# Gates and branch projections with tokens in the partitions and 512 weight columns a product

## The chip, the cores and the metric

The kernel runs on one core of one Trainium2 chip. The metric is device time of one execution in microseconds (us). The core's engines are TensorE (PE in the profile; PEld is its weight load), VectorE (DVE), ScalarE (ACT), GpSimd (POOL) and SyncE (SP), which here only issues DMAs. Each engine works through its own queue in order; engines wait for one another by semaphores.

## What is computed

One layer of a hybrid backbone over 256 latent tokens (and a prefix of 256 context tokens) with 2048 channels, in fp32. Cut to the part around the change:

```python
D_MODEL, SEQ, D_FF = 2048, 256, 5632          # h_l: 256 x 2048
def merge(h, ya, yb):
    g_a, g_b = jnp.split(jax.nn.sigmoid(h @ w_gate + b_gate), 2, axis=-1)     # w_gate 2048 x 4096
    return (g_a * (ya @ w_proj_gla) + g_b * (yb @ w_proj_diff)) @ w_out       # 1024 x 2048 each; 2048 x 2048
...
mix_l = merge(h_l, gla_out(o_lf + flip(o_lb), gr_l), diff_out(o_diff))
x_new = x + g1 * mix_l
h2_l = modulate(rms_norm(x_new, norm2_w), sh2, sc2)
x_new = x_new + g2 * conv_ffn(h2_l, w_up, conv_w, conv_b, w_down)
```

Ahead of it stand the modulation vectors (`silu(c) @ w_ada`), the input projection, a chunked gated linear attention (its output is `ya`) and a differential attention of eight heads (its output is `yb`).

## The kernel before, in words

**Products.** Every fp32 operand of a large product is split into a rounded high half and the low rest, and a product is made of three: high by high, low by high, high by low. `split` (L207 to L229) does it for a tile of 128x1024 weights: ScalarE copies the high half (L212), VectorE subtracts to get the low half (L219; now and then POOL does). `fetch` (L231) loads the raw tile on SP's queue. There are four raw buffers and three of each half.

**Two forms.** In the column form, `col_tile` (L244 to L278), a 128x128 tile of weights is stationary and the tokens move. The activations lie as [high | low] of 2 x 256 tokens, so the high weights take one product of 512 columns (L270) and the low weights one of 256 (L272). The result has output channels in the partitions, its two 256-column parts still to be added. In the row form, `row_tile` (L284 to L287), 128 tokens are stationary and 512 weight columns move, in three products of 512 columns. The dv part of the input projection (names `dvb`, L285 to L287) and the last product, down (L1386), are in row form; nearly all else is in column form.

**Order.** The kernel is written with a scheduler that simulates the engines and sets the order of each queue; attention has a high priority (L1132, L1136), so its products stand between those of the gates. Where a table or a list forces an order, `after` ties two instructions.

**Gates.** The loop over the eight heads (L1131 to L1151) makes three gate tiles per head in between attention's work, and the rest behind it: 32 tiles, `gate_tile` (L1116 to L1124). Each is one `col_tile` over 16 contraction tiles; ScalarE moves one half of the bank out and adds the gate bias by channel (L1123), VectorE adds the other half (L1124). `GATE_ADA` (L49) says how many modulation steps (`ada_next`, a VectorE dot of 128x1024, L371) go with each.

**Merge.** The projection loop (L1176 to L1193) runs over 16 channel tiles: two column tiles (`pga`, `pgb`), a sigmoid of the two gates (L1181), evacuation (`added`, L281 on ScalarE, L282 on VectorE), multiplication by the gate (L1187, for one branch on VectorE and for the other on POOL), and in `merged` the sum (L1172) and its split (L237, L238) into the places that the output projection reads. The mix loop (L1216 to L1240) is the output projection in column form.

**Places.** `C` are the places of the gates. They are cut from the places of the odd tiles of the high and low activations, which POOL copies away first by a DMA behind each step of the second dv chunk (`X4`, L1045).

Of the kernel before, what the change touches and what calls it, by code (L numbers as in the profile page):

```python
# [18 lines left out]
P = 128  # L19
D = 2048  # L20
# [33 lines left out]
for _n, _w in [("b_ada", 96), ("norm1", 16), ("norm2", 16), ("ba", 8), ("gonorm", 1), ("qnorm", 1),  # L54
               ("knorm", 1), ("donorm", 1), ("b_gate", 32), ("lam", 256), ("conv_w", 3 * 2 * FT),
               ("conv_b", 2 * FT)]:
    _VEC[_n] = (_o, _w)
    _o += _w
# [21 lines left out]
def _lay_out(i):  # L80
# [20 lines left out]
    a["w_in"] = _tiles(w_in, starts)  # L101
    a["w_gate"] = _tiles(np.asarray(i["w_gate"])[0], range(0, 2 * D, P))
    pg, pd = np.asarray(i["w_proj_gla"])[0], np.asarray(i["w_proj_diff"])[0]
    a["w_proj"] = _tiles(np.concatenate([pg, pd], axis=0), range(0, D, P))
    a["w_out"] = _tiles(np.asarray(i["w_out"])[0], range(0, D, P))
# [19 lines left out]
        "donorm": np.asarray(i["diff_onorm_w"])[0][:, None],  # L125
        "b_gate": _vec_tiles(np.asarray(i["b_gate"])[0]),
        "conv_w": np.asarray(i["conv_w"])[0].reshape(3, 2 * FT, P).transpose(2, 0, 1).reshape(P, -1),
# [25 lines left out]
def layer_kernel(tc, I, out):  # L153
# [3 lines left out]
    with es:  # L157
# [853 lines left out]
        with tc.tile_pool(name="diff", bufs=1) as pd:  # L1011
# [11 lines left out]
            def dv_chunk(j):  # L1023
# [7 lines left out]
                for q in turn:  # L1031
# [12 lines left out]
                    if j:  # L1044
                        nc.gpsimd.dma_start(X4[2 * q][:, 2:, :], A[2 * q + 1])  # L1045
                        A[2 * q + 1] = X4[2 * q][:, 2:, :]

            def dq_tile(h):
# [66 lines left out]

            def gate_tile(j):  # L1116
                ada_next(GATE_ADA[len(gates)])
                b = acc_bank("gate")
                col_tile(I["w_gate"][j], A, b)
                if j == len(C):  # L1120
                    C.append(shared(2 * (j // 2) + 1, j % 2, "C").rearrange("p (a t) -> p a t", a=2))
# [8 lines left out]
            dv_chunk(1)  # L1130
            order = [j for k in range(KT) for j in (k, KT + k)]  # L1131
# [18 lines left out]
            while order:  # L1150
                gate_tile(order.pop(0))  # L1151

# [6 lines left out]
        for p in range(NPAIR):  # L1159
# [9 lines left out]
        yap, ybp = [[y[h].rearrange("p (a b) -> p a b", a=2) for h in range(HEADS)] for y in (ya, yb)]  # L1169

        def merged(c, earlier):
            i = V.tensor_tensor(gates[c], gates[c], gates[16 + c], op=ALU.add)  # L1172
            after(i, earlier)
            split_act(A[c][:, 1, :], A[c][:, 0, :], gates[c])

        for c in range(KT):  # L1176
            ba, bb = acc_bank("pga"), acc_bank("pgb")
            col_tile(I["w_proj"][c, :, 0:8, :], yap, ba)
            col_tile(I["w_proj"][c, :, 8:16, :], ybp, bb)
            for j in (c, 16 + c):  # L1180
                sigs.append(S.activation(gates[j], gates[j], AF.Sigmoid))  # L1181
                after(sigs[-1], sigm)
                after(sigs[-1], copied[0])
            for b, j in ((ba, c), (bb, 16 + c)):
                t = p3.tile([P, T], F32, tag="pt", bufs=2, name="pt")
                i = added(t, b)
                (G if j > c else V).tensor_tensor(gates[j], t, gates[j], op=ALU.mult)  # L1187
                if j == c and c:
                    merged(c - 1, i)
            if c < KT - 2:  # L1190
                ada_next(13 / (KT - 2))
        merged(KT - 1, i)
        ada_done(0)  # L1193

# [7 lines left out]
        def unnormed(k, product, summed):  # L1202
# [10 lines left out]
            after(i, product)  # L1213

        half = KT // 2
        for c in range(KT):  # L1216
            b = acc_bank("mix")
            if 0 < c < half:
                ada_next(1)
            col_tile(I["w_out"][c], A, b)  # L1220
            if c == half:
# [213 lines left out]
```

## Time and profile before

| | us |
|---|---|
| median of 3 runs (lowest 1675.17, highest 1676.67) | 1675.4 |
| the profiled execution | 1675.7 |
| its span, first to last instruction | 1673.9 |
| TensorE busy | 1657.2 |
| VectorE busy | 1279.7 |
| ScalarE busy | 898.4 |
| POOL busy | 338.7 |

The chain of work that ended last is 90% TensorE's. By the first and last start of their products, the gates lie at 527.6 to 758.1 us, up to 694 us between attention's products, the branch projections at 758.3 to 847.9, the output projection (mix) at 848.2 to 937.8, up at 973.6 to 1429.5 and down at 1429.6 to 1668.8.

How to read it: the profile records one execution. A duration on PE is from the issue of a product to a modelled end, so that those of successive products overlap; what a stream of products takes is seen in their starts. "Idle before" names the instruction whose end released the engine. Durations of one instruction are in ns, times in us.

### The profile page before, as it was taken

Reading aid. Unit: us, or ns where it says so; the run is one execution under the profiler, and the core shown is the slowest. Engines: PE = TensorE matmul, PEld = TensorE weight load, DVE = VectorE, ACT = ScalarE, POOL = GpSimd, SP = SyncE. Lnnn points to the kernel's source line nnn. Section 1 sums busy time; section 2 is a strip of 40 time slices with the busy share of each in tenths; the row PEclk is TensorE's granted clock in tenths of the full one; section 3 lists DMA queues with packets and bytes.
Section 4 is the critical chain, followed back from the end, with each engine's and each line's share of the span. In section 5 each row is a group of like instructions: output and inputs, shape, how many; then the busy total and the mean of one; then the engine's idle time right before and its main releaser. Section 6 shows DMA issues by size and latency. Waiting matters only on the chain.

```text
span 1673.9 us, 25645 instructions
## 1 busy us (share of the span) xinstructions
PE 1657.2 (99%) x9476; PEld 1409.6 (84%) x9476; DVE 1279.7 (76%) x2013; ACT 898.4 (54%) x1475; POOL 338.7 (20%) x412
## 2 busy tenths in 40 slices
PE   9999999999999999999999999999999999999998
PEld 6679888788878888888888998888888888888887
DVE  5887877768678888788888797888888888744544
ACT  5235355654456776556655575555555555433332
POOL 0011332415011000002214101221222122684000
PEclk9999999999999999999999999999999999999999
DMA  9996735336665556687877666777777676777764
GB/s 384 408 363 218 228 129 172 113 120 199 200 218 179 187 192 195 226 289 259 270 270 232 178 202 208 238 229 232 237 240 240 220 236 214 209 220 207 219 192 136
DMA packets 111965, 372.74 MB, mean 223 GB/s; under 512 B 14560, under 2 KB 19680, under 8 KB 111840
## 3 DMA queue, kind: packets, MB, share of 16 engines
q1 hardware_dynamic: 102112, 362.51, 66.3%
q0 software_dynamic: 5696, 4.24, 1.0%
q10 hardware_dynamic: 4032, 4.37, 0.8%
q8 instruction: 74, 1.21, 0.3%
q14 instruction: 51, 0.42, 0.1%
HBM read 364.73 MB, written 2.10 MB: 219 GB/s over the span
## 4 chain that ended last, share of the span: by engine, by line
PE 90%; DVE 4%; DMA 3%; ACT 1%; POOL 1%; issue 1%; DVEq 0%; SPq 0%; ACTq 0%
PE down L1386 14%; PE upg L270 9%; PE upv L270 9%; PE gate L270 7%; PE upv L272 5%; PE upg L272 5%; PE sweep L383 4%; PE gate L272 4%; PE mix L270 4%; PE mix L272 2%; PE pga L270 2%; PE pgb L270 2%; PE dvb L285 1%; PE dvb L287 1%; PE dvb L286 1%; PE dq L270 1%
## 5 line engine op out<-in xcount | busy, mean ns | idle before, releaser
L212 ACT CAST whi<-wraw 128x1024 fp32r<-128x1024 f32 (+3 forms) x502 | 514.5, 1028 | 420.6 <-PE down L1386 138.9
L219 DVE TENSOR_TENSOR wlo<-wraw,whi 128x1024 fp32r<-128x1024 f32 (+3 forms) x466 | 562.9, 1209 | 205.7 <-ACT whi L212 200.5
L270 PE MATMUL upg<-x,whi 128*128 128x512 f32 x656 | 229.4, 392 | 0.0
L270 PE MATMUL upv<-x,whi 128*128 128x512 f32 x656 | 229.4, 392 | 0.0
L1386 PE MATMUL down<-whi,g 128*128 128x512 f32 x704 | 216.8, 389 | 0.0
L272 PE MATMUL upv<-x,wlo 128*128 128x256 f32 x656 | 183.0, 280 | 0.0
L272 PE MATMUL upg<-x,wlo 128*128 128x256 f32 x656 | 182.8, 280 | 0.0
L270 PE MATMUL gate<-x,whi 128*128 128x512 f32 x512 | 179.8, 398 | 0.0
L371 DVE CUSTOM_DVE_ANT_0 araw<-araw,cb 128x1024 f32<-128x1024 f32 x128 | 161.2, 1263 | 14.2 <-DMA araw<-in_w_ada 14.0
L219 POOL TENSOR_TENSOR wlo<-wraw,whi 128x1024 fp32r<-128x1024 f32 x36 | 86.8, 2411 | 396.3 <-ACT whi L212 396.3
L1386 PEld LDWEIGHTS down<-whi,g 128*128 128x128 f32 x704 | 132.1, 188 | 27.3
L270 PEld LDWEIGHTS upv<-x,whi 128*128 128x128 f32 x656 | 122.4, 187 | 26.8
L270 PEld LDWEIGHTS upg<-x,whi 128*128 128x128 f32 x656 | 122.4, 187 | 26.8
L272 PE MATMUL gate<-x,wlo 128*128 128x256 f32 x512 | 140.7, 285 | 0.2 <-DVE wlo L219 0.2
L1386 PE MATMUL down<-wlo,g 128*128 128x512 f32 x352 | 137.0, 389 | 0.0
L1297 DVE SCALAR_TENSOR_TENSOR C<-C,vec 128x255 f32<-128x255 f32 x88 | 105.5, 1201 | 36.8 <-ACT C L1296 36.8
L272 PEld LDWEIGHTS upv<-x,wlo 128*128 128x128 f32 x656 | 124.0, 189 | 0.5
L272 PEld LDWEIGHTS upg<-x,wlo 128*128 128x128 f32 x656 | 124.0, 189 | 0.5
L270 PEld LDWEIGHTS gate<-x,whi 128*128 128x128 f32 x512 | 94.3, 188 | 19.9 <-issue 0.7
L272 PEld LDWEIGHTS gate<-x,wlo 128*128 128x128 f32 x512 | 96.4, 189 | 5.6 <-issue 2.6
L270 PE MATMUL mix<-x,whi 128*128 128x512 f32 x256 | 88.8, 396 | 0.0
L1386 PEld LDWEIGHTS down<-wlo,g 128*128 128x128 f32 x352 | 66.1, 188 | 13.8
(332 smaller groups left out, 3239.8 us busy)
## 6 DMA issues: line engine op xcount, KB each, us to landing
wraw<-in_w_up SPq DMA_DIRECT2D x164, 512.0 KB, 4.6
araw<-in_w_ada SPq DMA_DIRECT2D x128, 512.0 KB, 5.6
wraw<-in_w_down SPq DMA_DIRECT2D x88, 512.0 KB, 4.2
wraw<-in_w_gate SPq DMA_DIRECT2D x64, 512.0 KB, 4.5
wraw<-in_w_in SPq DMA_DIRECT2D x58, 512.0 KB, 4.7
ada<-in_w_ad SPq DMA_DIRECT2D x52, 512.0 KB, 9.9
wraw<-in_w_proj SPq DMA_DIRECT2D x32, 512.0 KB, 4.7
wraw<-in_w_out SPq DMA_DIRECT2D x32, 512.0 KB, 5.0
```

Source lines behind the costliest of these rows:

```text
L212: copied[0] = S.copy(hi[:, :n], raw)
L219: i = e.tensor_tensor(lo[:, :n], raw, hi[:, :n].bitcast(F32), op=ALU.subtract)
L270: i = PE.matmul(b.rearrange("p (a b) -> p a b", a=2), whi[:, sl], acts[k], start=first, stop=last)
L272: i = PE.matmul(b[:, T:], wlo[:, sl], acts[k][:, 1, :], start=False, stop=last)
L285: PE.matmul(o, hi[k][:, ts], whi[:, sl], start=first, stop=False)
L286: PE.matmul(o, lo[k][:, ts], whi[:, sl], start=False, stop=False)
L287: return PE.matmul(o, hi[k][:, ts], wlo[:, sl], start=False, stop=last)
L371: i = V.tensor_tensor_reduce(raw, raw, cb[:, q * 1024:(q + 1) * 1024], 1.0, 0.0, op0=ALU.mult, op1=ALU.add, accum_out=ada2[:, j, q:q + 1])
L383: return kept(PE.matmul(*args, **kw))
L1297: V.scalar_tensor_tensor(u[:, 1:], b[:, :T - 1], vcol("conv_w", ct), u[:, 1:], op0=ALU.mult, op1=ALU.add)
L1386: i = PE.matmul(banks[h][t][n], g[:, a, ts], w[n][b], start=k == 0 and (a, b) == (1, 0), stop=k == FT - 1 and b == 1)
```

## The change

The gates and the two branch projections are turned from column form to row form.

- **Gates:** 64 steps (`gate_step`) of one 128x1024 tile, which now holds 512 output channels of two contraction tiles. Eight steps fill two banks of 128 tokens x 512 channels, a chunk; there are eight chunks, a and b branch alternating. A step is 12 products of 512 columns (two contraction tiles, two token tiles, three each). Each head gets six steps.
- **Gate bias:** it is now along the free dimension. A broadcast DMA on SP's queue puts 512 bias values into all partitions of the gate's place, [128, 2, 512], and VectorE adds the bank to it at the chunk's end. The bias leaves the vector that is loaded at the start.
- **Projections:** four chunks of 512 channels, two branches each, in row form. VectorE multiplies a bank by the gate (128x512); the sum of the branches is made by POOL for the first three chunks and by VectorE for the last.
- **Turn:** the sum has tokens in the partitions, and the output projection wants channels there. TensorE transposes it in blocks of 128x128, four to a bank (`turned`); ScalarE and VectorE split the result into the output projection's places. Chunks 0 to 2 are turned during the next chunk; the last is turned behind the first part of the first two tiles of mix, which are now written out by hand (`mix_part`).
- The number of modulation steps in each stage is unchanged. The weights are laid out in memory to match.

```diff
-GATE_ADA = [0.25] * 4 + [0.5] * 16 + [1] * 12
+GATE_ADA = [0.125] * 8 + [0.25] * 32 + [0.5] * 24
...
-            def gate_tile(j):
-                ada_next(GATE_ADA[len(gates)])
-                b = acc_bank("gate")
-                col_tile(I["w_gate"][j], A, b)
...
-                gates[j] = C[j % KT][:, j // KT, :]
-                S.activation(gates[j], b[:, :T], AF.Identity, bias=vcol("b_gate", j))
-                V.tensor_tensor(gates[j], b[:, T:], gates[j], op=ALU.add)
+            def gate_step():
+                n, q = divmod(gate_at[0], 8)
+                ada_next(GATE_ADA[gate_at[0]])
+                gate_at[0] += 1
+                if q == 0:
+                    banks[n] = [acc_bank("gate") for _ in range(2)]
+                    gates[n] = [shared(2 * n + 1, t, "C") for t in range(2)]
+                    nc.sync.dma_start(taken[2 * n + 1, "C"].rearrange("p (a b) -> p a b", a=2),
+                                      I["b_gate"][n].to_broadcast([P, 2, 512]))
+                flush(latest if latest else later)
+                both = split(fetch(I["w_gate"][n, q].rearrange("p a b -> p (a b)"), 1024), 1024)
+                for a in range(2):
+                    k = 2 * q + a
+                    w = [h[:, a * 512:(a + 1) * 512] for h in both]
+                    for t in range(2):
+                        row_tile(banks[n][t], k, *w, slice(0, 512), H[0][0], H[0][1], slice(t * P, (t + 1) * P), k == 0, k == KT - 1)
+                if q == 7:
+                    for t in range(2):
+                        V.tensor_tensor(gates[n][t], banks[n][t], gates[n][t], op=ALU.add)
...
-                for _ in range(3):
-                    gate_tile(order.pop(0))
+                for _ in range(6):
+                    gate_step()
...
-        def merged(c, earlier):
-            i = V.tensor_tensor(gates[c], gates[c], gates[16 + c], op=ALU.add)
-            after(i, earlier)
-            split_act(A[c][:, 1, :], A[c][:, 0, :], gates[c])
-
-        for c in range(KT):
-            ba, bb = acc_bank("pga"), acc_bank("pgb")
-            col_tile(I["w_proj"][c, :, 0:8, :], yap, ba)
-            col_tile(I["w_proj"][c, :, 8:16, :], ybp, bb)
...
+        def turned(c, t):
+            b = aux_bank("turn", t)
+            for j in range(4):
+                PE.transpose(b[:, j * P:(j + 1) * P], gates[2 * c][t][:, j * P:(j + 1) * P], ident)
+            ts = slice(t * P, (t + 1) * P)
+            for j in range(2):
+                o = b[:, j * T:(j + 1) * T].rearrange("p (a t) -> p a t", a=2)
+                x = X4[4 * c + 2 * j]
+                S.copy(x[:, 1::2, ts], o)
+                V.tensor_tensor(x[:, 0::2, ts], o, x[:, 1::2, ts].bitcast(F32), op=ALU.subtract)
...
+        for c in range(4):
+            for branch in range(2):
+                bs = [acc_bank("pg") for _ in range(2)]
+                n = 2 * c + branch
+                ws = []
+                for q in range(4 * branch, 4 * branch + 4):
+                    both = split(fetch(I["w_proj"][c, q].rearrange("p a b -> p (a b)"), 1024), 1024)
...
+                    if q % 4 == 1:
+                        sigmoids(n)
+                    if n > 1 and q in (1, 2):
+                        turned(c - 1, q - 1)
+                for t in range(2):
+                    for k, w in ws:
+                        row_tile(bs[t], 0, *w, slice(0, 512), *[[h] for h in Y[k]], slice(t * P, (t + 1) * P), k % 8 == 0, k % 8 == 7)
+                    V.tensor_tensor(gates[n][t], bs[t], gates[n][t], op=ALU.mult)
+                    if branch:
+                        (G if c < 3 else V).tensor_tensor(gates[n - 1][t], gates[n - 1][t], gates[n][t], op=ALU.add)
...
+        heads = [acc_bank("mix") for c in range(2)]
+        for c in range(2):
+            mix_part(c, heads[c], mix_halves(c, 0), 0, 8)
+        late = []
+        for c in range(2):
+            late.append(mix_halves(c, 8))
+            mix_part(c, heads[c], late[c], 8, 12)
+        for t in range(2):
+            turned(3, t)
+        for c in range(2):
+            mix_part(c, heads[c], late[c], 12, 16)
```

What the scheduler makes of it, at three places. First TensorE's queue at the head of the gates, before (`x_277` and so on are the places of the activations, `s` is attention's scores):

```order
L270 MATMUL gate<-x_277,whi 128x512
L1076 MATMUL s<-ks,qs 128x512 x6
L272 MATMUL gate<-x_277,wlo 128x256
L270 MATMUL gate<-x_277,whi 128x512
L272 MATMUL gate<-x_277,wlo 128x256
L270 MATMUL gate<-x_419,whi 128x512
L272 MATMUL gate<-x_419,wlo 128x256
```

And the same place after (`pT` are attention's transposes, `hss` sums of squares):

```order
L1082 MATMUL s<-ks,qs 128x512 x6
L1107 MATMUL pT<-ident,pe 128x128 x4
L290 MATMUL gate<-whi,x_277 128x512
L291 MATMUL gate<-whi,x_277 128x512
L290 MATMUL gate<-whi,x_277 128x512
L291 MATMUL gate<-whi,x_277 128x512
L652 MATMUL hss<-wlo,bones 128x256
L653 MATMUL hss<-whi,bones 128x256
L292 MATMUL gate<-wlo,x_277 128x512 x2
L290 MATMUL gate<-whi,x_277 128x512
L291 MATMUL gate<-whi,x_277 128x512
L292 MATMUL gate<-wlo,x_277 128x512
```

Pairs of 512 and 256 columns have become threes of 512, and in the first contraction tile of a step the products of the low weights stand last, behind four of the high ones.

Second, TensorE's queue where the first half of a chunk is turned, in the projections of the next chunk (`ya` are the a branch's activations, `C` the merged sum), after:

```order
L292 MATMUL pg<-wlo,ya_7187 128x512
L290 MATMUL pg<-whi,ya_7194 128x512
L291 MATMUL pg<-whi,ya_7194 128x512
L1194 MATMUL turn<-ident,C 128x128 x4
L292 MATMUL pg<-wlo,ya_7194 128x512
L290 MATMUL pg<-whi,ya_7194 128x512
L291 MATMUL pg<-whi,ya_7194 128x512
```

Before, the corresponding stretch of TensorE's queue has products alone:

```order
L270 MATMUL pga<-ya_7486,whi 128x512
L272 MATMUL pga<-ya_7486,wlo 128x256
L270 MATMUL pga<-ya_7489,whi 128x512
L272 MATMUL pga<-ya_7489,wlo 128x256
L270 MATMUL pga<-ya_7496,whi 128x512
```

Four transposes that read POOL's sum have come between the products; the first such group stands 26 products behind the end of its chunk.

Third, VectorE's queue in the projections, before (`pt` is an evacuated bank, L371 the modulation dot):

```order
L282 TENSOR_TENSOR pt<-pgb,pt 128x256
L219 TENSOR_TENSOR wlo<-wraw,whi 128x1024
L282 TENSOR_TENSOR pt<-pga,pt 128x256
L1172 TENSOR_TENSOR C<-C 128x256
L1187 TENSOR_TENSOR C<-pt,C 128x256
L219 TENSOR_TENSOR wlo<-wraw,whi 128x1024
L371 ISA araw,ada_77<-araw,cb 128x1024
```

And after:

```order
L224 TENSOR_TENSOR wlo<-wraw,whi 128x1024 x3
L376 ISA araw,ada_77<-araw,cb 128x1024
L376 ISA ada_77 128x1
L224 TENSOR_TENSOR wlo<-wraw,whi 128x1024
L1231 TENSOR_TENSOR C<-pg,C 128x512 x2
L224 TENSOR_TENSOR wlo<-wraw,whi 128x1024
L376 ISA araw,ada_77<-araw,cb 128x1024
```

The evacuations and sums of 256 columns are gone from it; two multiplications of 512 columns, one for each bank of a chunk, stand together behind low halves of the steps that follow.

Last, SP's queue at the end of the dv stage, after (before, the same weight and modulation loads stand there without the bias):

```order
L1132 DMA C<-in_b_gate 128x2x512
L238 DMA wraw<-in_w_in 128x1024
L370 DMA araw<-in_w_ada 128x1024
L1132 DMA C<-in_b_gate 128x2x512
L238 DMA wraw<-in_w_gate 128x1024
```

Six of the eight bias loads have come between the last loads of the input projection and the first of the gates; the other two stand among later gate loads.

## Rows read from the trace of the kernel before

**Rows 1.** The page: TensorE's busy us, share and instructions; granted clock in 40 slices.

```profile
PE 1657.2 (99%) x9476; PEld 1409.6 (84%) x9476; DVE 1279.7 (76%) x2013; ACT 898.4 (54%) x1475; POOL 338.7 (20%) x412
...
PEclk9999999999999999999999999999999999999999
```

**Rows 2.** Waits of TensorE, 520 to 940 us: total, times, longest us.

```profile
PE gate L272 <- DVE wlo L219: 0.2, 1, 0.2
```

**Rows 3.** Line L270: ns min/median/max, first and last start us, shapes.

```profile
L270 PE MATMUL gate<-x,whi x512: 387/396/501, 527.6 to 758.1; 128*128 128x512 f32 x171
L270 PE MATMUL mix<-x,whi x256: 387/396/404, 848.2 to 937.8; 128*128 128x512 f32 x128
L270 PE MATMUL pga<-ya,whi x128: 392/397/401, 758.3 to 845.1; 128*128 128x512 f32 x128
```

**Rows 4.** Line L1386 (down), the same columns.

```profile
L1386 PE MATMUL down<-whi,g x704: 387/389/397, 1429.6 to 1668.5; 128*128 128x512 f32 x176
...
L1386 PE MATMUL down<-wlo,g x352: 388/389/398, 1430.0 to 1668.8; 128*128 128x512 f32 x176
```

**Rows 5.** Windows: length, busy us (records) by engine, clock, DMA share, GB/s.

```profile
706.00:756.00 50.00, 50.00 (x285) 43.44 (x284) 40.45 (x60) 28.46 (x43) 0.00 (x0) 1.00 0.87 289
760.00:840.00 80.00, 80.00 (x458) 69.79 (x457) 70.80 (x119) 49.57 (x98) 20.41 (x14) 1.00 0.81 268
...
560.00:580.00 20.00, 20.00 (x117) 16.68 (x117) 19.47 (x36) 15.05 (x28) 2.42 (x2) 1.00 0.64 213
```

**Rows 6.** Timeline of TensorE in the dv stage: start us, us, line, operation.

```profile
486.94 0.40 PE L285 MATMUL dvb<-whi,x 128*128 128x512 f32 x1
...
489.45 0.39 PE L287 MATMUL dvb<-wlo,x 128*128 128x512 f32 x1
```

**Rows 7.** Timeline of TensorE around a group of attention's transposes.

```profile
612.24 0.40 PE L270 MATMUL gate<-x,whi 128*128 128x512 f32 x1
612.47 0.28 PE L272 MATMUL gate<-x,wlo 128*128 128x256 f32 x1
612.59 0.60 PE L1101 MATMUL pT<-ident,pe 128*128 128x128 f32 x4
612.95 0.48 PE L270 MATMUL gate<-x,whi 128*128 128x512 f32 x1
613.26 0.28 PE L272 MATMUL gate<-x,wlo 128*128 128x256 f32 x1
613.38 0.39 PE L270 MATMUL gate<-x,whi 128*128 128x512 f32 x1
```

**Rows 8.** VectorE's groups, 520 to 940 us: busy us, mean ns, idle before.

```profile
L219 DVE TENSOR_TENSOR wlo<-wraw,whi 128x1024 fp32r<-128x1024 f32 x135 | 169.5, 1258 | 34.7 <-ACT whi L212 31.6 <-PE gate L272 1.9
...
L1124 DVE TENSOR_TENSOR C<-gate,C 128x256 f32<-128x256 f32 x32 | 13.4, 420 | 4.2 <-ACT C L1123 4.1
...
L1164 DVE TENSOR_TENSOR ge<-oy,ge 128x512 f32<-128x512 f32 x4 | 2.8, 689 | 0.0
```

**Rows 9.** Timeline of POOL's copy and SP's next gate load.

```profile
503.95 0.53 POOL L1045 DMA_DIRECT2D x<-x  x1 [5.81 <-PE dvb L287]
...
510.27 0.33 SPq L233 DMA_DIRECT2D wraw<-in_w_gate  x1
```

**Rows 10.** Line L1045, POOL's eight copies: from issue to landing.

```profile
DMA to landing us min/median/max: 2.3/5.7/7.2
```

**Rows 11.** Timelines of TensorE, two windows before the gates: stalls behind splits.

```profile
454.16 0.50 PE L270 MATMUL dq<-x,whi 128*128 128x512 f32 x1 [0.55 <-ACT whi L212]
...
468.18 0.50 PE L285 MATMUL dvb<-whi,x 128*128 128x512 f32 x1 [0.76 <-ACT whi L212]
```

**Rows 12.** Timeline of all engines in the gates: a low half and its reader.

```profile
588.34 1.23 DVE L219 TENSOR_TENSOR wlo<-wraw,whi 128x1024 fp32r<-128x1024 f32 x1 [0.52 <-ACT whi L212]
...
590.23 0.28 PE L272 MATMUL gate<-x,wlo 128*128 128x256 f32 x1
```

**Rows 13.** Line L1187 on POOL: ns min/median/max, first and last start us.

```profile
L1187 POOL TENSOR_TENSOR C<-pt,C x16: 733/1654/1659, 765.1 to 850.3; 128x256 f32<-128x256 f32 x16
```

More of the change, by code (lines that the diff above doesn't have):

```diff
@@ L101, in _lay_out, with chunks @@
     a["w_in"] = _tiles(w_in, starts)
-    a["w_gate"] = _tiles(np.asarray(i["w_gate"])[0], range(0, 2 * D, P))
+    def chunks(w, order):
+        w = w.reshape(KT // 2, 2, P, -1, 512)
+        return np.ascontiguousarray(w.transpose(3, 0, 2, 1, 4)[order])
+    order = [j for c in range(4) for j in (c, 4 + c)]
+    a["w_gate"] = chunks(np.asarray(i["w_gate"])[0], order)
+    a["b_gate"] = np.ascontiguousarray(np.asarray(i["b_gate"])[0].reshape(8, 1, 1, 512)[order])
     pg, pd = np.asarray(i["w_proj_gla"])[0], np.asarray(i["w_proj_diff"])[0]
-    a["w_proj"] = _tiles(np.concatenate([pg, pd], axis=0), range(0, D, P))
+    a["w_proj"] = chunks(np.concatenate([pg, pd], axis=0), list(range(4)))
     a["w_out"] = _tiles(np.asarray(i["w_out"])[0], range(0, D, P))
@@ L1147, in layer_kernel @@
                     dq_tile(4 + h)
-                for _ in range(3):
-                    gate_tile(order.pop(0))
-            while order:
-                gate_tile(order.pop(0))
+                for _ in range(6):
+                    gate_step()
+            while gate_at[0] < 64:
+                gate_step()
         p3 = r2.enter_context(tc.tile_pool(name="merge", bufs=1))
@@ new lines, in layer_kernel @@
+        Y = [(y[h][:, T:], y[h][:, :T]) for y in (ya, yb) for h in range(HEADS)]
+        def turned(c, t):
[8 more added lines that the diff above has]
+                V.tensor_tensor(x[:, 0::2, ts], o, x[:, 1::2, ts].bitcast(F32), op=ALU.subtract)
@@ L1182, in layer_kernel, with sigmoids @@
+        def sigmoids(n):
+            for t in range(2):
+                sigs.append(S.activation(gates[n][t], gates[n][t], AF.Sigmoid))
                 after(sigs[-1], sigm)
                 after(sigs[-1], copied[0])
[L1184 to L1189, printed above, removed]
@@ L1190, in layer_kernel @@
[L1190 to L1192 removed]
+        for c in range(4):
[5 more added lines that the diff above has]
+                    both = split(fetch(I["w_proj"][c, q].rearrange("p a b -> p (a b)"), 1024), 1024)
+                    for a in range(2):
+                        ws.append((2 * q + a, [h[:, a * 512:(a + 1) * 512] for h in both]))
+                    if c < 3:
+                        ada_next(13 / 24)
+                    if n < 7 or q < 6:
+                        for k, w in ws:
+                            for t in range(2):
+                                row_tile(bs[t], 0, *w, slice(0, 512), *[[h] for h in Y[k]], slice(t * P, (t + 1) * P), k % 8 == 0, k % 8 == 7)
+                        ws = []
+                    if q % 4 == 1:
+                        sigmoids(n)
+                    if n > 1 and q in (1, 2):
+                        turned(c - 1, q - 1)
+                for t in range(2):
+                    for k, w in ws:
+                        row_tile(bs[t], 0, *w, slice(0, 512), *[[h] for h in Y[k]], slice(t * P, (t + 1) * P), k % 8 == 0, k % 8 == 7)
+                    V.tensor_tensor(gates[n][t], bs[t], gates[n][t], op=ALU.mult)
+                    if branch:
+                        (G if c < 3 else V).tensor_tensor(gates[n - 1][t], gates[n - 1][t], gates[n][t], op=ALU.add)
@@ L1213, in unnormed, with mix_part, mix_halves @@
             after(i, product)
+        def mix_part(c, b, w, k0, k1):
+            for k in range(k0, k1):
+                sl = slice(k % 8 * P, (k % 8 + 1) * P)
+                PE.matmul(b.rearrange("p (a b) -> p a b", a=2), w[0][:, sl], A[k], start=k == 0, stop=False)
+                PE.matmul(b[:, T:], w[1][:, sl], A[k][:, 1, :], start=False, stop=k == KT - 1)
+        def mix_halves(c, k0):
+            return split(fetch(I["w_out"][c, :, k0:k0 + 8, :].rearrange("p a b -> p (a b)"), 1024), 1024)
+        heads = [acc_bank("mix") for c in range(2)]
[5 more added lines that the diff above has]
+            mix_part(c, heads[c], late[c], 8, 12)
+        for t in range(2):
+            turned(3, t)
+        for c in range(2):
+            mix_part(c, heads[c], late[c], 12, 16)
         half = KT // 2
         for c in range(KT):
-            b = acc_bank("mix")
+            b = heads[c] if c < 2 else acc_bank("mix")
             if 0 < c < half:
                 ada_next(1)
-            col_tile(I["w_out"][c], A, b)
+            if c > 1:
+                col_tile(I["w_out"][c], A, b)
             if c == half:
```

12 lines of the change are left out of this document (4 added, 8 removed).

## Prediction, made before the changed kernel was run

> **What bounds the kernel now.** I began with the granted clock and the page's engine table: TensorE is busy for 1657.2 us, 99% of the span, with the full clock granted in every slice [rows 1]. Then I read what TensorE waits for in the stretch that the change touches, from 520 to 940 us: one wait of 0.2 us, and nothing else [rows 2]. So in the gates, the branch projections and the output projection, TensorE never starves; no stall can be removed there, and only TensorE's own issue time can be won. VectorE, ScalarE and the queues matter in one way alone: they may be made late enough to stop TensorE.
>
> The next view is where each product starts first and last [rows 3, 4]. A trap stands in it: durations of pipelined products overlap (a 512-column product reads 0.39 us while the next starts 0.23 us after it), so the price of a product is the distance from start to start, never its mean duration.
>
> **The price of the two forms.** *Column form (before).* A pair is one 512-column product and one 256-column product. The projections hold 256 pairs between 758.3 us, their first, and 848.2 us, where mix begins: 89.9 / 256 = 351 ns [rows 3]. In the stretch 706 to 756, in which PE runs gates alone, 285 records are 142.5 pairs in 50 us: 351 ns; 760 to 840 gives 80 / 229 = 349 ns [rows 5]. *Row form (after).* Down is written in that form: tokens stationary, 512 weight columns moving. Its 704 + 352 products start between 1429.6 and 1668.8 us: 239.2 / 1055 = 226.7 ns [rows 4]. The dv stage runs the very function that the change calls; there twelve products start over 2.51 us: 228 ns [rows 6].
>
> A unit of 128 contraction rows by 256 weight columns is two pairs in column form, 702 ns, and three products in row form, 680 ns. (Both are 1536 moving columns; column form loses because half of its instructions are short.) So a unit gives back 22 ns. The gates have 256 units (512 pairs): 5.6 us. The projections have 128: 2.8 us. **Together 8.4 us won**, all on TensorE and so on the path. Bounds: with the pair at 349 and the product at 228, a unit gives 14 ns and the sum is 5.4 us; with the pair at 352 (the same window less one record) and the product at 226.7 it gives 24 ns, 9.2 us.
>
> **What is added on TensorE.** The merged sum now has tokens in the partitions and must be turned: 32 transposes of 128x128, in groups of four. The trace has such groups, attention's pT. Between the gate product at 612.24 and that at 613.38 stand two pairs and one group: 1.14 us, less 0.70 for the pairs: 0.44 us for a group, changeover included [rows 7]. The low end is the group's own distance to the next product, 612.59 to 612.95: 0.36. The product behind the group takes 0.31 instead of 0.23, and if the one before it lost as much the group would cost 0.52. Eight groups: **3.5 us added** (2.9 to 4.2).
>
> Order is the same elsewhere: mix keeps its products, but the first two of its tiles are now opened ahead of the last turn, as cover. That moves products and adds none.
>
> The Trainium skill ("TensorE: Matmul & The Clock Gate", section "Back-to-back issue gap") gives a product of N columns N / 2.4 + 2.5 ns when warm. By that a unit would be 650 ns before and 648 after, and the change would lose by its transposes; the rows read 702 and 680 instead, so they don't bear it out here.
>
> **What is moved off TensorE, costed at nothing.** ScalarE loses 32 bias activations and 32 evacuations and gains 16 small casts; it had room already. On VectorE 32 adds of 256 columns at 0.42 us in the gates become 16 of 512 columns; the nearest row for that size is 0.69 us [rows 8], so 13.4 us become 11. The projections' adds, products and sums of 256 columns likewise become 512-wide ones with less work in total. VectorE was at 40.45 of 50 us in the gates and 70.80 of 80 in the projections [rows 5], so it keeps its spare. What is new is their order: at a chunk's end the two 512-wide operations stand in VectorE's queue and wait for TensorE's last products, and the next low half of a weight tile stands behind them. TensorE waits for that half. In the order the low halves of the two following steps are already ahead of the pair; a step is 12 products, 2.7 us, so the cover is 5.4 us against 2 x 0.69 = 1.4 us of work plus a low half of 1.26 [rows 8]. I take zero.
>
> The gate bias becomes eight transfers of 512 KB on SP's queue. Six of them stand between weight loads at the end of the dv stage, and each waits until POOL's copy has cleared the place it writes. Copies took 5.7 us (7.2 at most) to land; the one issued at 503.95 lands near 509.65, and the weight load behind it was issued at 510.27 anyway [rows 9, 10]. With the slowest landing, 511.15, the load would go 0.9 us late, and the four raw buffers hold more than two steps of work, some 5.4 us. Zero again; without that cover it would be six times 0.9, 5.4 us.
>
> **The sum.** The profiled execution took 1675.7 us (span 1673.9 plus 1.8 around it), 0.3 above the median of 1675.4. 1675.7 - 8.4 + 3.5 = 1670.8; against the median, 1670.5. I say 1670.6. TensorE's terms alone allow -9.2 + 2.9 = -6.3 to -5.4 + 4.2 = -1.2, that is 1669.1 to 1674.2.
>
> **The rivals.**
>
> *VectorE is late at chunk ends (slower).* There are 16 chunk ends, eight in the gates and eight in the projections; six lie in the attention stage, where VectorE was busy 19.47 of 20 us in 560 to 580 [rows 5], and where the order puts four high products and then the low ones. In such stretches before the gates, where splits ran behind, TensorE stood 0.55 and 0.76 us at one product [rows 11]. At 0.76 at each of 16 ends, 12.2 us are lost: 1683. It decides from (3.35 + 4.9) / 16 = 0.52 us per end, above which the kernel is measurably slower. Against it: the closest low half I found in the gates ended at 589.57, 0.66 us before TensorE asked for it at 590.23 [rows 12], others lead by more, and the work falls. 0.13.
>
> *The turn waits for POOL (no change).* The sums of the first three chunks are 512-wide additions on POOL. Its 256-wide product took 0.73 to 1.66 us [rows 13], so a 512-wide one 1.5 to 3.3. The first turn of a chunk stands 26 products, 5.9 us, behind the chunk's last product, the second 8.6 us. They need 0.69 + 3.3 = 4.0 us and 1.4 + 6.6 = 8.0 us by the slow price: just hidden. If POOL falls behind by what the early load of VectorE and ScalarE gave, 0.55 to 0.76 us, at six groups, 3.3 to 4.6 us are lost: 1673.8 to 1675.1. A late bias load (5.4 us, 1675.9) ends in the same place. 0.20 together.
>
> *The two forms cost the same by the column here (doesn't do what it says).* Both move 1536 columns a unit. If the longer distance of the short instructions came from this stage's weight traffic, and not from their being short, the row form would inherit it: TensorE gains nothing and pays 3.5 us: 1678.9, slower. Against it: the column form reads 349 to 351 ns in two stages, and the row form 227 to 228 in two others under different loads [rows 3 to 6]. The Trainium skill's formula, weighed above, comes out close to this: 1.0 us won for 3.5 paid, 1677.9. 0.07, of which 0.03 is for the formula's version.
>
> **How the numbers follow.** A measurement of this kernel tells about 0.2%, 3.35 us, from no change. My forecast has 0.60; most of it lies below 1672.05 and counts as faster, except the corner where a dearer row product (228) or cheap pairs meet dear transposes (0.05). The POOL and bias case (0.20) is no change; the VectorE rival and the last one (0.20) are slower, less 0.04 for light forms of the first that stay within the bound. So faster 0.55, no change 0.29, slower 0.16. The range runs from 1668.0, a little under TensorE's best sum, to 1678.5, which takes in the POOL case and light stalls and leaves out the heavy VectorE case.
>
> **What would show it.** Right: 768 gate and 384 projection products that start 227 to 228 ns apart; eight turn groups at about 0.44 us; gates plus projections plus turns about 4.9 us shorter, with up and down unchanged; TensorE's waits from 520 to 940 still near zero; six POOL additions that end before their turns. Wrong: waits of TensorE on the low half behind VectorE's 512-wide operations; turns that stand for POOL; weight loads late behind a bias load; product distances other than 227, or a granted clock below 1.00.

## The result: slower, where faster was forecast

| | median us | runs | lowest to highest | ratio to the kernel before (95% interval) |
|---|---|---|---|---|
| before | 1675.79 | 6 | 1674.92 to 1676.72 | |
| changed | 1682.12 | 6 | 1680.76 to 1684.33 | 1.0038 (1.0025 to 1.0051) |

The change costs 6.3 us where 4.9 us were to be won: 11.2 us lie between. The profiled execution of the changed kernel took 1684.3 us, 2.2 above its median; that of before took 1675.7.

The page of the changed kernel says as little against it as that of before [rows 1] (span; busy us, share of the span, instructions):

```profile
span 1682.5 us, 24760 instructions
...
PE 1660.0 (99%) x9124; PEld 1394.6 (83%) x9124; DVE 1266.7 (75%) x1951; ACT 879.2 (52%) x1395; POOL 322.6 (19%) x402
```

TensorE is still 99% busy, VectorE and ScalarE have less work. What is new is in the waits of TensorE, here from 480 to 960 us (engine, line, awaited; us in total, times, longest). Before, the stretch from 520 on held one wait of 0.2 [rows 2]:

```profile
PE dq L275 <- DMA x<-x: 1.9, 1, 1.9
PE hss L652 <- DVE wlo L224: 1.6, 2, 1.3
PE gate L290 <- ACT whi L217: 1.2, 1, 1.2
PE o L1113 <- ACT pT L1108: 0.7, 1, 0.7
```

The first and last starts by line tell the stages (ns min/median/max, then first and last start in us), as in [rows 3, 4]:

```profile
L290 PE MATMUL gate<-whi,x x256: 387/389/580, 535.1 to 763.0; 128*128 128x512 f32 x128
...
L290 PE MATMUL pg<-whi,ya x64: 389/396/478, 763.7 to 843.6; 128*128 128x512 f32 x64
...
L1260 PE MATMUL mix<-x,whi x32: 389/395/403, 855.5 to 870.0; 128*128 128x512 f32 x32
...
L275 PE MATMUL upg<-x,whi x656: 389/391/403, 982.2 to 1432.3; 128*128 128x512 f32 x164
...
L1450 PE MATMUL down<-whi,g x704: 387/389/397, 1438.2 to 1677.1; 128*128 128x512 f32 x176
```

| stage, from the first start to that of the next, us | before | changed | difference | forecast |
|---|---|---|---|---|
| up to the projections | 758.3 | 763.7 | +5.4 | -5.6 |
| projections (with six of eight turns) | 89.9 | 91.8 | +1.9 | -0.2 |
| mix and the first part of up (with two turns) | 125.4 | 126.7 | +1.3 | +0.9 |
| rest of up | 456.0 | 456.0 | 0 | 0 |
| down, to its last start | 239.2 | 239.2 | 0 | 0 |

So the gates' stretch lost most, the projections some, and what the change doesn't touch is the same. Of the 5.4 us up to the projections, 1.4 may be chance: TensorE waited that long at a product of the linear attention (L949, near 429 us), and a second profile of the same kernel, below, has no such wait there. Where the gates run alone, the price of a gate product is what was forecast: 18 products start from the first of these two rows to the second, 4.08 / 18 = 227 ns (timeline of TensorE: start us, us, line, operation):

```profile
729.72 0.39 PE L290 MATMUL gate<-whi,x 128*128 128x512 f32 x1
...
733.80 0.39 PE L290 MATMUL gate<-whi,x 128*128 128x512 f32 x1
```

A turn, too, costs what attention's transposes cost [rows 7]. Between the two outer products below stand one product and one group: 0.91 us, less two distances of 0.23, is 0.45:

```profile
791.82 0.40 PE L291 MATMUL pg<-whi,ya 128*128 128x512 f32 x1
792.05 0.60 PE L1194 MATMUL turn<-ident,C 128*128 128x128 f32 x4
792.41 0.48 PE L292 MATMUL pg<-wlo,ya 128*128 128x512 f32 x1
792.73 0.40 PE L290 MATMUL pg<-whi,ya 128*128 128x512 f32 x1
```

A projection product is dearer. From the first to the second row below are 20 products: 4.65 / 20 = 232.5 ns.

```profile
765.09 0.40 PE L290 MATMUL pg<-whi,ya 128*128 128x512 f32 x1
...
769.74 0.39 PE L290 MATMUL pg<-whi,ya 128*128 128x512 f32 x1
```

The first of the waits has consequences. POOL's last copy was issued at 520.9 and TensorE stood 1.90 us for it, while SP's queue stood at the bias load that waits for the same copy (timelines of TensorE and of SP's queue):

```profile
526.67 0.28 PE L277 MATMUL dq<-x,wlo 128*128 128x256 f32 x1
528.86 0.67 PE L275 MATMUL dq<-x,whi 128*128 128x512 f32 x1 [1.90 <-DMA x<-x]
529.32 0.41 PE L277 MATMUL dq<-x,wlo 128*128 128x256 f32 x1
529.54 0.63 PE L275 MATMUL dq<-x,whi 128*128 128x512 f32 x1
```

```profile
519.45 0.38 SPq L1132 DMA_DIRECT2D C<-in_b_gate  x1
520.62 0.33 SPq L238 DMA_DIRECT2D wraw<-in_w_gate  x1
528.87 0.38 SPq L1132 DMA_DIRECT2D C<-in_b_gate  x1
529.34 8.49 SPq L238 DMA_DIRECT2D wraw<-in_w_gate  x3
```

The gate weights behind that bias load were issued at 529.34; before, that load went out at 522.5. Right after its wait TensorE ran at the lower of its two levels (1.2 instead of 2.4 GHz): a pair took 0.64 us instead of 0.35, and the window says a mean granted clock of 0.54 (length, busy us by engine, clock, DMA share, GB/s):

```profile
528.80:532.50 3.70, 3.64 (x12) 2.83 (x14) 1.42 (x5) 0.83 (x2) 1.04 (x2) 0.54 0.31 107
```

### The profile page after: what moved, and what is told of

Read it like the earlier page. It is cut to its first block, busy times and chain, and to the rows that moved or that the text cites. A ratio compares the mean times of both kernels' runs of the same rounds, so it can differ in the third digit from the quotient of the medians.

```text
span 1682.5 us, 24760 instructions
## 1 busy us (share of the span) xinstructions
PE 1660.0 (99%) x9124; PEld 1394.6 (83%) x9124; DVE 1266.7 (75%) x1951; ACT 879.2 (52%) x1395; POOL 322.6 (19%) x402
## 4 chain that ended last, share of the span: by engine, by line
PE 91%; DVE 4%; ACT 2%; DMA 2%; issue 1%; POOL 1%; DVEq 0%; ACTq 0%
PE down L1450 14%; PE upg L275 9%; PE upv L275 9%; PE sweep L388 6%; PE upv L277 5%; PE upg L277 5%; PE gate L292 4%; PE gate L290 3%; PE gate L291 3%; PE mix L275 3%; PE pg L290 2%; PE pg L292 2%; PE pg L291 2%; PE dvb L290 2%; PE dvb L292 2%; PE dvb L291 2%
## 5 line engine op out<-in xcount | busy, mean ns | idle before, releaser
L290 PE MATMUL gate<-whi,x 128*128 128x512 f32 x256 | 101.3, 396 | 1.2 <-ACT whi L217 1.2
L291 PE MATMUL gate<-whi,x 128*128 128x512 f32 x256 | 100.4, 392 | 0.0
L292 PE MATMUL gate<-wlo,x 128*128 128x512 f32 x256 | 95.6, 394 | 0.1
L275 PE MATMUL mix<-x,whi 128*128 128x512 f32 x224 | 77.9, 397 | 0.0
L1423 POOL DMA_DIRECT2D row<-turned x128 | 69.5, 551 | 29.3 <-issue 18.9
```

Of the source, the lines that this page charges most:

```text
L275: i = PE.matmul(b.rearrange("p (a b) -> p a b", a=2), whi[:, sl], acts[k], start=first, stop=last)
L290: PE.matmul(o, hi[k][:, ts], whi[:, sl], start=first, stop=False)
L291: PE.matmul(o, lo[k][:, ts], whi[:, sl], start=False, stop=False)
L292: return PE.matmul(o, hi[k][:, ts], wlo[:, sl], start=False, stop=last)
L1423: nc.gpsimd.dma_start(to[32 * (q % 4):32 * (q % 4 + 1), :, 32 * p:32 * (p + 1)], turned[32 * p:32 * (p + 1), :, 32 * q:32 * (q + 1)])
```

## Experiments

Two theories stood first. A: the bias loads among the last loads of the dv stage are the loss. B: the row form itself makes VectorE and ScalarE late in the attention stage.

### Bias loads issued late, left out, and added to the kernel before

```diff
-                    nc.sync.dma_start(taken[2 * n + 1, "C"]..., I["b_gate"][n]...)      # at q == 0
+                if q == 4:
+                    i = nc.sync.dma_start(taken[2 * n + 1, "C"]..., I["b_gate"][n]...)
+                    after(i, copied[0])
```

> The changed kernel, with each bias load issued at the fifth step of its chunk, behind POOL's copies, and nothing else altered. Theory A (bias loads among the last loads of the dv stage hold SP's queue and make POOL's last copy late, so TensorE waits 1.9 us, its clock drops, and the first gate weights come late): the wait on the copy near 528 us and the wait for the first gate's high half near 535 us vanish, the granted clock of 520 to 540 us is 1.00, and the time is 1672 to 1676. Theory B (the row form itself makes VectorE's and ScalarE's work late in the attention stage): waits on low halves and on attention's transposes near 565, 594 and 621 us stay, and the time is 1680 or more.

The second kernel has no bias load, and its last operation of a chunk is a copy:

```diff
-                        V.tensor_tensor(gates[n][t], banks[n][t], gates[n][t], op=ALU.add)
+                        V.tensor_copy(gates[n][t], banks[n][t])
```

> The changed kernel without the gate bias: no bias load, and at a chunk's end VectorE copies the bank instead of adding (same size). Theory A: within 1 us of the run with late bias loads, 1672 to 1676, and no wait near 528. Theory B: 1680 or more, the waits from 535 to 625 us stay. What it is below the run with late loads is the price of eight well placed loads.

The third is the kernel before with the loads alone:

```diff
                     C.append(shared(2 * (j // 2) + 1, j % 2, "C")...)
+                    if j % 2 == 0:
+                        nc.sync.dma_start(taken[j + 1, "C"]..., I["b_row"][j // 2].to_broadcast([P, 2, 512]))
```

> The kernel before, with the eight broadcast bias loads added into the gates' places ahead of the gates' own writes (which overwrite them), at the same positions of SP's queue as in the changed kernel. All else is as before. Theory A: slower than before by 3 to 8 us, TensorE waits on POOL's last copy near 528 us and the granted clock drops there. Theory B: within 1 us of before.

Measured: late loads 1681.43 us, ratio 1.0035 (1.0022 to 1.0047); no loads 1680.75, 1.0031 (1.0020 to 1.0042); before with the loads 1677.78, 1.0014 (1.0005 to 1.0024). With late loads the wait on the copy and the low clock are gone, and the waits that theory B names are all still there (waits of TensorE, 380 to 960 us):

```profile
PE hss L652 <- DVE wlo L224: 1.6, 2, 1.3
PE gate L290 <- ACT whi L217: 1.5, 1, 1.5
...
PE o L1113 <- ACT pT L1108: 0.7, 1, 0.7
```

So A is right that the loads make the copy late, and wrong on the size: put late, the loads give back 0.7 us of the median, and left out 1.4, both within the intervals of the three kernels; added to the kernel before they cost 2.0, which is clear of its interval, with this row, in which TensorE waits 1.32 us for the same copy:

```profile
528.40 0.50 PE L271 MATMUL dq<-x,whi 128*128 128x512 f32 x1 [1.32 <-DMA x<-x]
```

The low clock that A forecast didn't come with it: the pairs behind this wait take 0.35 us. A second profile of the changed kernel (the run of 2080 bytes, below) says the same. Its wait for the copy was 1.72 us and the granted clock stayed at 1.00 from 520 to 540 us; it fell later, behind a wait for a low half of the head's norm (timeline of TensorE, then the window):

```profile
564.42 0.39 PE L652 MATMUL hss<-wlo,bones 128*128 128x256 f32 x1 [1.26 <-DVE wlo L224]
```

```profile
565.00:570.00 5.00, 4.94 (x14) 3.60 (x15) 5.00 (x7) 3.73 (x7) 0.00 (x0) 0.66 0.47 155
```

So the fall isn't tied to the bias loads. By the mean clock of the two windows TensorE lost some 1.7 us each time (0.46 of 3.70 us, 0.34 of 5.00).

### The place of the deferred norm work

What was late then? ScalarE's queue tells it. In the order of the kernel before, the copy of the first gate weights stands right behind the start of a head's norm (`hny`); in the changed one it stands behind the whole norm, attention's softmax (`pe`) and the start of the next head's norm (`nraw`, `nsq`). The number in front is the place in the queue. Before:

```
404 L309 ACTIVATE hny<-hss,epsb 128x256
405 L212 CAST whi<-wraw 128x1024
406 L312 ACTIVATE hny<-hny 128x256
```

Changed:

```
404 L314 ACTIVATE hny<-hss,epsb 128x256
405 L317 ACTIVATE hny<-hny 128x256
406 L318 ACTIVATE nsq<-hny 128x256
407 L1108 COPY pT<-pT 128x4x128
408 L1092 ACTIVATE pe,sm<-s,sm 128x512 x2
409 L1103 ACTIVATE pe<-pe,sm 128x512
410 L286 COPY nraw<-dq 128x256
411 L242 CAST qs<-dq 128x256
412 L661 ACTIVATE nsq<-nraw 128x256
413 L217 CAST whi<-nsq 128x256
414 L217 CAST whi<-wraw 128x1024 x2
```

The weights were not late: without bias loads they were issued at 503.2 us, as before. One line of the change orders it so: `gate_step` calls `flush(latest if latest else later)`, which writes out the deferred norm work of the attention heads, ahead of the step's load and split. `col_tile` does that in its second half, behind its first split and first eight contraction tiles. Theory C: the place of this call costs the time, not the form of the products.

```diff
-                flush(latest if latest else later)
                 both = split(fetch(I["w_gate"][n, q]...), 1024)
                 for a in range(2):
+                    if a:
+                        flush(latest if latest else later)
```

> The kernel with late bias loads, and the deferred norm work of the attention heads is written out in the middle of a gate step, behind the step's split and its first contraction tile, instead of ahead of both (before, the column tile had it in its second half). Theory C (the place of the deferred work puts ScalarE's copy of the first gate weights and VectorE's low halves behind norm work they need not wait for): the 1.5 us wait of the first gate product goes, those of the sums of squares on a low half (1.3 and 0.3) shrink, and the time falls by 3 to 6 us against the run with late bias loads, to about 1676 to 1678. Theory B (row form itself): waits and time stay within 1 us of that run.

> As the run with the deferred work in the middle of the step, but written directly behind the split and ahead of all products. Theory C, if only the split's place matters: the same time within 1 us. If the products' place matters too: the first gate's wait goes, but the waits of the sums of squares stay, about 2 us more.

Measured (both with late bias loads): in the middle 1675.88 us, ratio 1.0001 (0.9991 to 1.0010); right behind the split 1675.81, 1.0001 (0.9992 to 1.0011). That is 5.5 us below the same kernel with the call in front, and level with the kernel before. ScalarE's copy of the first gate weights is back at 523.19, ahead of the rest of the norm, and the waits on the high half and on the low half of the norm are gone (timeline of ScalarE, then waits of TensorE, both with the call in the middle):

```profile
522.82 0.47 ACT L314 ACTIVATE hny<-hss,epsb 128x256 f32<-128x256 f32 x1
523.19 1.03 ACT L217 CAST whi<-wraw 128x1024 fp32r<-128x1024 f32 x1
524.13 0.41 ACT L317 ACTIVATE hny<-hny 128x256 f32<-128x256 f32 x1
```

```profile
PE dq L275 <- ACT whi L217: 1.0, 2, 0.5
PE o L1113 <- ACT pT L1108: 0.9, 2, 0.6
```

Waits of 0.9 us for attention's transposes remain; the kernel before has none of them. The two places of the call give the same time, so what counts is that the weights' load and split come first. The call alone, moved in the changed kernel with its early bias loads:

> The changed kernel with only the deferred norm work moved to the middle of the gate step; the bias loads stay among the last loads of the dv stage. Theory C alone: 5.5 us below the changed kernel, 1676 to 1677, so the bias loads' place costs at most 1 us. If the bias loads' place costs what it did beside the kernel before (2.0): 1677.5 to 1678.5. A wait on POOL's last copy near 528 us stays in the trace.

Measured: 1677.45 us, ratio 1.0011 (1.0001 to 1.0021), with a wait of 1.6 us on POOL's copy and no low clock behind it. That is above what C alone forecast. So the call gives 4.7 us, and the bias loads' place 1.6 beside it, the latter between two intervals that overlap a little. The counter-test puts the early call into the kernel before, in column form:

```diff
             for k0 in range(0, nk, 8):
                 kn = min(8, nk - k0)
-                if k0:
+                if early:
+                    flush(latest if latest else later)
+                elif k0:
                     flush()
                 raw = fetch(...)
...
-                col_tile(I["w_gate"][j], A, b)
+                col_tile(I["w_gate"][j], A, b, early=True)
```

> The kernel before, column form, with only one thing altered: in the gates the deferred norm work is written out ahead of each half tile's load and split, at the same points as in the changed kernel. Theory C (the place of the deferred work costs, whatever the form): 4 to 6 us slower than before, 1679 to 1682, with a first gate product that waits on ScalarE's high half and sums of squares that wait on a low half. If only the row form suffers from it: within 1 us of before.

Measured: 1688.24 us, ratio 1.0075 (1.0060 to 1.0090): 12.6 us for the same call, two to three times the forecast. TensorE's waits from 380 to 960 us:

```profile
PE gate L272 <- ACT whi L212: 5.0, 4, 1.5
PE gate L274 <- DVE wlo L219: 2.1, 4, 0.6
```

The first gate product waits on the high half as forecast; the other waits are at gate products too, and not at sums of squares. They are 7.1 us together, against 3.8 in the row form with the call in front (late bias loads). Behind the first of them the clock fell here as well, and the window shows some 1.7 us lost to it:

```profile
530.00:540.00 10.00, 8.78 (x39) 7.49 (x40) 8.26 (x16) 7.78 (x15) 0.00 (x0) 0.83 0.53 163
```

The mean clock of the four executions was 0.996 to 0.998, lower than the 0.999 to 1.000 of the changed kernel, so a part of the 12.6 us is the clock's; how much in the median was not measured. C stands on its direction and B falls: the column form suffers from that call as well, and its waits are the longer ones.

### Why a projection product is dearer

> The changed kernel with the places of the projections' activations 2080 bytes apart instead of 2064. Only the projections' product distance is looked at (231 to 235 ns in the changed kernel, 227 in its gates). If the places' alignment is the cause: 227 ns, and the projection stage, 91.8 us, gets 2 us shorter. If the cause is another: 231 to 235 stays.

This run told nothing of that: in the memory map of the built kernels (the start address of each tile) 2064 bytes are rounded up to 2080, so the two kernels are the same. It serves as a second profile of the changed kernel: projections from 764.0 to 855.7, 91.7 us, with products of 231 to 235 ns, and 1684.2 us in all.

```diff
-        Y = [(y[h][:, T:], y[h][:, :T]) for y in (ya, yb) for h in range(HEADS)]
+        Y = [(H[0][0][h], H[0][1][h]) for h in range(2 * HEADS)]
```

> The kernel with late bias loads; the projections take the activations of the gates (other places in SBUF) as stationary operands instead of the two branches' outputs, so that their results are not those of the layer; sizes, order and all else are the same. If the place or the values of the stationary operand make a projection product 231 to 235 ns: 227 ns and a projection stage 2 us shorter than 91.5. If not: unchanged.

Measured: the stage takes 850.9 - 761.0 = 89.9 us, 1.8 less than with late bias loads alone (759.3 to 851.0):

```profile
L290 PE MATMUL pg<-whi,x x128: 387/389/478, 761.0 to 850.3; 128*128 128x512 f32 x128
...
L1262 PE MATMUL mix<-x,whi x32: 387/398/403, 850.9 to 865.6; 128*128 128x512 f32 x32
```

Then the same values in the usual places:

```diff
-                split_act(ya[h][:, T:], ya[h][:, :T], e[:, j * T:(j + 1) * T])
+                S.copy(ya[h][:, T:], H[0][0][h])
+                V.tensor_copy(ya[h][:, :T], H[0][1][h])
```

> The kernel with late bias loads; the places of the two branches' outputs are filled with copies of the gates' activations (ScalarE and VectorE copies instead of the split), so that the projections read the usual places with other values; their results are not those of the layer. If the place makes a projection product 231 to 235 ns: unchanged, projection stage 91.5 us. If the values do: 227 ns and 89.9 us, as with the gates' activations in their own places.

Measured: 760.9 to 852.6, 91.7 us, and a median duration of 396 as in the changed kernel. So it is the places and not the values. The memory map gives a candidate. All tiles of the gates' activations start at the same offset within 512 bytes (480); those of the projections lie 2080 bytes apart in memory, so that their offsets differ from tile to tile by multiples of 32.

```diff
-                ya[h] = p2.tile([P, 2 * T + 4], F32R, tag=tag, name=f"ya{h}")[:, :2 * T]
+                ya[h] = p3.tile([P, 2 * T], F32R, tag=f"ya{h}", name=f"ya{h}")
```

> The kernel with late bias loads and the deferred work in the middle of the step; the eight stationary tiles of the first branch get places of their own, 2048 bytes apart and at the same offset within 512 bytes as the activations of the gates (those of the second branch stay 2080 apart, at changing offsets). Order and sizes are the same. If the offset within 512 bytes sets the distance of a projection product: 227 ns in the first branch, 231 to 235 in the second, projection stage 0.9 us shorter (90.9 us), time 1675. If the region of memory does: first branch 231 to 235 as well, no change.

Measured: in the first chunk of the first branch 20 products start from the first of these rows to the second, 4.54 / 20 = 227 ns; by line, its median duration is 389 now and that of the second branch 396 as ever:

```profile
755.38 0.39 PE L290 MATMUL pg<-whi,ya 128*128 128x512 f32 x1
...
759.92 0.39 PE L290 MATMUL pg<-whi,ya 128*128 128x512 f32 x1
```

```profile
L290 PE MATMUL pg<-whi,ya x64: 387/389/478, 754.0 to 833.3; 128*128 128x512 f32 x64
L290 PE MATMUL pg<-whi,yb x64: 388/396/404, 764.9 to 844.4; 128*128 128x512 f32 x64
```

The stage falls to 845.1 - 754.0 = 91.1 us, 0.6 of the 0.9 us forecast. The time is 1675.62 us, ratio 0.9999 (0.9990 to 1.0008): a gain of 0.3 us against the run with the call in the middle, which the measurement can't tell from none.

The offset of a tile by itself is not the cause, though. In the same run, on the same tiles, eight products between two turns start 1.86 / 8 = 232 ns apart:

```profile
782.64 0.40 PE L290 MATMUL pg<-whi,ya 128*128 128x512 f32 x1
...
784.50 0.39 PE L292 MATMUL pg<-wlo,ya 128*128 128x512 f32 x1
```

Nor is it the region. In the changed kernel the first tile of the first branch lies at offset 480 too, in the usual region; behind the gates its products start 0.91 / 4 = 227 ns apart, and the 20 products of the next tiles, shown above, 232.5:

```profile
763.72 0.39 PE L290 MATMUL pg<-whi,ya 128*128 128x512 f32 x1
...
764.63 0.62 PE L292 MATMUL pg<-wlo,ya 128*128 128x512 f32 x2
```

What the slower stretches have in common is that the offset of the stationary tiles had just changed or that a turn had come shortly before; in the stretches read here where neither happened, the distance is 227. (A change by 256 bytes alone, to the first tile of the second branch in this run, left it at 227.) What TensorE does there stays open, and no run used another common offset.

## Why the prediction was wrong, step by step

- **The forms' prices: right where the gates run alone.** 227 ns a product, as [rows 4, 6] said. Over the whole stage the row form won less than the 5.6 us forecast: in the trace of the kernel before, the distances from each gate product to the next product add up to 183.0 us, and in the run with the call in the middle, waits taken off, to 178.5. That is 4.5 us; the rest goes where attention's products stand between those of the gates. The Trainium skill's formula ("TensorE: Matmul & The Clock Gate", section "Back-to-back issue gap"), which the section gives for an isolated product, would make it 216 ns; no stage of these products ran at that.
- **The projections' 2.8 us: mis-sized.** The price was carried over from another stage. At 232.5 instead of 226.7 ns, 384 products cost 2.2 us more, and the row form won only some 0.6 us there. The places of the stationary tiles set it: with the gates' tiles in their stead the stage was 1.8 us shorter.
- **Eight turns, 3.5 us: right.** 0.45 us each.
- **"Order is the same elsewhere", and the work off TensorE at nothing: the step that failed.** The prediction compared how much work VectorE and ScalarE have, and took the operations at a chunk's end for all that is new in their order. It left out what stands ahead of the weights' split in their queues at the start of the gates, though the diff moves a call that decides it. ScalarE's row 405, the waits above and the runs that move the call show the result: it costs 4.7 us in the changed kernel, 5.5 beside late bias loads.
- **The bias loads at nothing: failed, and by another path.** The prediction let the copies delay a weight load, which the raw buffers would cover. But TensorE itself waits for the last copy. The prediction took the copies to land in 5.7 us and 7.2 at most [rows 10]; beside the bias loads they took longer, the last one some 8:

```profile
DMA to landing us min/median/max: 3.5/6.3/8.1
```

  The place of the loads costs 0.7 to 2.0 us by the medians of three comparisons (late against early, with and without the call moved; added to the kernel before), less than the 5.4 us given for lost cover. In the first profile it cost more, since the clock fell after the wait; in the second the clock fell elsewhere.
- **The rival "VectorE is late at chunk ends": its time was near the result by luck (1683 forecast at its high price, 1682.1 measured), its mechanism was not.** No wait of TensorE stands at a chunk end; VectorE's 512-wide additions took the forecast 0.68 us and on TensorE nothing but one weight load waited for them (0.4 us). The waits are at the heads' norms, with another cause.
- **The rival "the turn waits for POOL": did not happen.** POOL's additions took 1.3 to 2.3 us and no turn waited:

```profile
L1233 POOL TENSOR_TENSOR C<-C x6: 1289/1790/2287, 786.3 to 833.8; 128x512 f32<-128x512 f32 x6
```

The account: of the 11.2 us, the call and the bias loads are 6.2 together (1682.12 to 1675.88). The other 5 can be read from the profile of the run with both mended, which took 1675.9 us, its median:

```profile
L290 PE MATMUL pg<-whi,ya x64: 389/396/478, 755.6 to 835.6; 128*128 128x512 f32 x64
...
L1263 PE MATMUL mix<-x,whi x32: 389/395/403, 847.4 to 861.9; 128*128 128x512 f32 x32
...
L275 PE MATMUL upg<-x,whi x656: 389/391/403, 973.8 to 1423.9; 128*128 128x512 f32 x164
```

Up to the projections it is 2.7 us shorter than before where 5.6 were forecast. Of the 2.9 missing, 1.1 are the gate products (4.5 for 5.6), 0.9 the waits for attention's transposes, like the one below, and 0.9 a wait at L949 near 429 us, which comes and goes between executions (the run with the call right behind the split has none).

```profile
588.37 1.99 PE L1113 MATMUL o<-pT,dv 128*128 128x256 f32 x8 [0.56 <-ACT pT L1108]
```

The projections miss their forecast by 2.1, mix and the first part of up by 0.1. Executions of one kernel scatter by 2 to 4 us, and the profiled ones lie up to 2.2 us on either side of their median, so that such an account from one profile is no finer than that. No version was measurably faster than the kernel before: with the call and the loads mended and half of the projections' places, the change is worth nothing that can be measured.

## What to carry to other kernels

When a change rewrites a loop, look for the calls in it that write out deferred work, and compare each engine's queue at the first step of the new loop: where the weights' split stands against work that nobody waits for yet. A smaller sum of work on an engine says nothing of that; one line moved cost 4.7 us here, as much as the whole change was to bring. And a price read in one stage is safe for another only with the same places of the operands and the same neighbours.

## What the hardware showed that was not expected

- The projections' products of 512 columns started 227 ns apart or some 232, by the places of their stationary tiles, in the same order and also with the same values (227 with the gates' tiles, 232 with copies of them in the usual places). With one common offset they took 227 until a turn came, and 232 between two turns.
- Eight transfers of 512 KB, added to the kernel before, cost it 2.0 us though TensorE never waits for their data: it waited 1.32 us for a copy issued beside them.
- In the changed kernel a wait of 1.90 us was followed by a mean granted clock of 0.54 over 3.7 us. In its second profile a wait of 1.72 us at the same place was followed by the full clock, and one of 1.26 us elsewhere by a mean of 0.66 over 5 us. In the kernel before with bias loads the wait at the same place was 1.32 us, and the pairs behind it took 0.35 us as usual.
